# A gated hybrid layer: the first norm's 1/rms applied behind the projections, and x loaded already transposed

## The chip, the cores and the metric

The kernel runs on one core of one Trainium2 chip. The metric is the device time of one execution in microseconds (us). TensorE (PE in the profile) multiplies matrices, VectorE (DVE), ScalarE (ACT) and GpSimd (POOL) work on tiles, SyncE (SP) issues most of the transfers (DMAs).

## What is computed

One layer on x of 1024 tokens by 1024 channels, all in float32. Cut to what the change touches:

```python
h = rms_norm(x, norm1_w[l])
proj = h @ w_in[l]
q, k, v, g_ret, x_lru, y_lru, gate_ret, gate_lru = jnp.split(proj, SPLIT_POINTS, axis=-1)
q = rotary(q.reshape(bsz, seq, RET_HEADS, RET_DK), positions)
k = rotary(k.reshape(bsz, seq, RET_HEADS, RET_DK), positions) * (RET_DK ** -0.5)
o = chunkwise_retention(q, k, v.reshape(bsz, seq, RET_HEADS, RET_DV))
o = head_group_norm(o, ret_gn_w[l])
y_a = (o * jax.nn.silu(g_ret)) @ w_ret_o[l]
xc = causal_depthwise_conv(x_lru, lru_conv_w[l], lru_conv_b[l])
hl = rg_lru(xc, ...)
y_b = (hl * jax.nn.gelu(y_lru)) @ w_lru_o[l]
mix = (jax.nn.sigmoid(gate_ret + merge_gate_b[l, 0]) * y_a
       + jax.nn.sigmoid(gate_lru + merge_gate_b[l, 1]) * y_b)
x = x + mix @ w_out[l]
...
```

Behind these lines stand a second rms norm, a gated MLP with a short convolution, its residual and a final rms norm.

`rms_norm` is x * rsqrt(mean(x*x) + eps) * w, the mean over a row; `proj` has 7168 columns. Each row (token) of `h` is a row of x times one number, its 1/rms, and each column times a weight of the norm. A row's number can therefore multiply the product instead of x.

## The kernel before

**Numbers.** A float32 operand is split in two parts, hi and lo, of a shorter float type that TensorE takes in one pass: `split` (lines 167 and 168) casts hi on ScalarE and subtracts it on VectorE for lo. A product is three passes, hi by hi, hi by lo and lo by hi (`PASSES`).

**Jobs.** The first projection has 7168 columns. 256 of them make a job, so there are 28 jobs, in the order of `SEQ`: g is a merge gate, y the GeLU branch, h0 to h3 the four heads with three jobs each (q and k; v; the swish gate), x the LRU branch. A job has four weight blocks of 128 x 512 (`A11` to `A22`, column half and row half), and the operand `h1` has 32 tiles of 128 channels by 512 tokens, as 16 pairs of hi and lo: `B11` is the first four row tiles of channels and the first half of the tokens, `B12` the second half of the tokens, `B21` and `B22` the other four row tiles. The weights are the stationary side; the result has channels on the partitions and tokens along the row.

The first two jobs (`STD_L = 2`) are plain products, `mm_std`, of 96 matmuls (line 317): for each column half m it takes two PSUM banks, one for each half of the tokens. The others are `mm_fast`, which forms a job from seven smaller products of 12 matmuls (line 347) with sums of blocks: sums of weights are made by `preps` (S1 to S4, on VectorE, lines 235 to 251), and sums of the operand once by `tsets` (T1 to T4, lines 484 to 493), out of the unsplit tiles in `keep`. A fast job uses three banks, X, Y and Z; its partial results are copied out by ScalarE (line 362) and completed by VectorE (`total`, line 371).

**What a job does with its results.** `jb.emit(m, h, src, unit)` is called for each quarter. `src` is a PSUM bank or an SBUF tile (`unit`, then both are the same). `emit_gate` applies the sigmoid and stores, `emit_y` GeLU and stores, `emit_to` keeps a tile for the work behind (with a function for the swish gate). The work behind a job, retention, rotary, the LRU block, is a generator in `back`, which `advance` moves on between products.

**Order.** The program is written as one stream; a scheduler in the framework orders the instructions of each engine by priority (the place in the stream, moved ahead by 1500 inside `hp()`) and by the time at which it expects them to be ready. Each engine then works through its list in order. Weights are loaded (`loads`, line 197) and prepared (`preps`) ahead by `pump`, up to 7 prepared blocks. `Units` hands out the SBUF tiles of 2 KB a partition (`NU` of them in `u`, 22 in `w`) and the PSUM banks: six in `g` for products, two in `a` for everything else.

**The start.** x is loaded with tokens on the partitions (`xload`, line 503), eight tiles for each half of the tokens. `norm_half` forms the rows' 1/rms (`rms_scale`, squares on lines 440 and 442, the root and its refinement on lines 427 to 432), multiplies the tiles by it (line 455), transposes them on TensorE (line 462, with the identity out of `cst`), and makes from each transposed tile hi, lo and the unsplit tile, with the norm's weight as a scale for each partition (lines 466 to 472). The first half's norm uses all eight banks (`wide`) and stands ahead of the first job; the second half's comes into the first job's matmuls. The rotary tables are worked out on VectorE behind the second job (lines 541 to 600).

Of the kernel before, what the change touches and what calls it, by code (L numbers as in the profile page):

```python
# [11 lines left out]
F32 = mybir.dt.float32  # L12
# [74 lines left out]
class Units:  # L87
    """places of one shape in a pool, handed out oldest first in program order"""
# [23 lines left out]
NU = 78  # L112
# [16 lines left out]
def tile_trunk_layer(ctx, tc, x, positions, params, consts, normf, w_in, w_ro, w_lo,  # L129
# [34 lines left out]
    def split(src, get=get):  # L164
        """the two float32r parts of a float32 operand"""
        hi, lo = get(F32R), get(F32R)
        S.copy(hi, src)  # L167
        V.tensor_sub(lo, src, hi.bitcast(F32))  # L168
        return hi, lo
# [5 lines left out]
    ORD_T = ("A11", "A12", "A21", "A22")  # L175

    class Job:
        def __init__(self, src, op, emit, post=None, fast=False, last=False, drop12=False,
                     pre=None):
# [8 lines left out]
    def loads():  # L188
        i = 0
        while True:  # L190
            while i >= len(queue):
                yield None
            jb = queue[i]
            for nm in (("A11", "A21", "A22", "A12") if jb.fast else ORD_T):
# [18 lines left out]
    def preps():  # L213
        i = 0
        while True:
            while i >= len(queue):
                yield None
            jb = queue[i]

            def fin(nm, src):  # L220
                jb.blk[nm] = split(src, W.get)
                state["blocks"] += 1

            if not jb.fast:
                for nm in ORD_T:
# [110 lines left out]

    def mm_fast(jb, op):
# [56 lines left out]
    def run(jobs):  # L394
        if jobs[0] not in queue:
            queue.extend(jobs)
        pump()
        ahead = None
        for jb, nx in zip(jobs, jobs[1:] + [None]):
            state["hp"] = jb is not queue[0]  # L400
            if jb.fast:
# [9 lines left out]
                next(g, None)  # L411
            else:
# [21 lines left out]
    def rms_scale(tiles, n, o=0):  # L434
        """1 / rms of n token tiles, one column each"""
# [15 lines left out]
    def norm_half(tiles, wname, op, half, keep, wide=False):  # L451
# [4 lines left out]
        banks = [psg.get() for _ in range(len(psg))] if wide else []  # L456
        banks += [psa.get() for _ in range(len(psa))]
        for k in range(KT):
# [16 lines left out]
            if k + len(banks) >= KT:  # L475
                (psa if k % len(banks) >= len(banks) - 2 else psg).put(ps)
# [57 lines left out]
    rot = {}  # L534

    def rotary_tables():
# [55 lines left out]
        for hf in range(2):  # L592
# [13 lines left out]
    def emit_to(d, func=None):  # L606
        def emit(m, h, src, unit):
            t = get() if unit is None else unit
            if func is not None:
                S.activation(t, src, func)  # L610
            elif unit is None:
                S.copy(t, src)
            d[m, h] = t
        return emit

    def emit_y(n):
        def emit(m, h, src, unit):
            t = get() if unit is None else unit
            S.activation(t, src, AF.Gelu_apprx_tanh)
# [118 lines left out]
    def retention_head(hd, qk, vv):  # L738
        cur = 0
        mask = cst[:, C_MASK + 128 * hd:C_MASK + 128 * hd + 128]  # L740
        for h in range(2):
            for g in range(2):
# [7 lines left out]
                S.copy(t, ps)  # L750
# [64 lines left out]
    def emit_gate(which, n):  # L815
        def emit(m, h, src, unit):
            t = get() if unit is None else unit
            S.activation(t, src, AF.Sigmoid, bias=pc("merge_gate_b", 8 * which + 2 * n + m))
# [4 lines left out]
    def operand(op, fetch, sums=True):  # L823
        """the sets of an operand: first those of the plain product, then the sums"""
# [52 lines left out]
    def add(i, emit, post=None):  # L877
# [4 lines left out]
        jobs.append(Job(pair_src(w_in, i), h1, emit, post, fast=fastj(), drop12=len(jobs) == STD_L - 1))  # L882
# [7 lines left out]
    for what in SEQ.split():  # L890
# [5 lines left out]
        elif what[0] == "x":  # L896
            n = int(what[1])
            add(2 * n, emit_to(xl), lambda n=n: lru_block(n, dict(xl)))
        else:
# [4 lines left out]
            add(base + 2, emit_to(gg, AF.Silu), lambda hd=hd: ret_out(hd, dict(gg)))  # L904
# [22 lines left out]
    V.memset(st, 1.0)  # L927
    S.activation(st[:, 0:1], st[:, 1:2], AF.Sqrt)
# [8 lines left out]
    pump()  # L937
# [137 lines left out]
    def square(m, c):  # L1075
        """what a finished tile adds to its rows' sum of squares; then the norm's weights"""
# [40 lines left out]
def _pairs(w, cols):  # L1117
    """[pair, 2 * (column half) + row half, partition, (row tile, column)]"""
# [4 lines left out]
def _layout(inputs):  # L1123
# [8 lines left out]
    for n in range(8):  # L1132
# [8 lines left out]
        "x": c(a["x"][0]),  # L1141
        "positions": c(a["positions"]),
# [26 lines left out]
```

## Time and profile before

| | us |
|---|---|
| median of 3 runs | 1692.53 |
| lowest and highest run | 1690.29, 1696.99 |
| span of the profiled execution, first to last instruction | 1689.3 |
| TensorE busy in it | 1634.8 |
| VectorE busy | 1253.0 |
| ScalarE busy | 882.4 |
| mean granted TensorE clock | 0.992 |

The profile records one execution. No time of its own stands beside its span; the fastest timed run is 1.0 us above the span and the median 3.2 us. In the profile an instruction group is named by its line, its engine, the operation and `out<-in`; numbers of buffers are left out, so `u` is any of the 2 KB tiles, `g` a product bank, `w` a weight tile, `a` one of the two other banks. A matmul's duration (0.39 us) is longer than the distance to the next one, because they overlap in the array; the distance sets the pace.

### The profile page before, as it was taken

Reading aid. Unit: us, or ns where it says so; the run is one execution under the profiler, and the core shown is the slowest. Engines: PE = TensorE matmul, PEld = TensorE weight load, DVE = VectorE, ACT = ScalarE, POOL = GpSimd, SP = SyncE. Lnnn points to the kernel's source line nnn. Section 1 sums busy time; section 2 is a strip of 40 time slices with the busy share of each in tenths; the row PEclk is TensorE's granted clock in tenths of the full one; section 3 lists DMA queues with packets and bytes.
Section 4 is the critical chain, followed back from the end, with each engine's and each line's share of the span. In section 5 each row is a group of like instructions: output and inputs, shape, how many; then the busy total and the mean of one; then the engine's idle time right before and its main releaser. Section 6 shows DMA issues by size and latency. Waiting matters only on the chain. (4 is left out here: it accounts for less than half of the span.)

```text
span 1689.3 us, 21180 instructions
## 1 busy us (share of the span) xinstructions
PE 1634.8 (97%) x7284; PEld 1341.8 (79%) x7284; DVE 1253.0 (74%) x2295; ACT 882.4 (52%) x1464; POOL 40.7 (2%) x60
## 2 busy tenths in 40 slices
PE   6999999999999999999999999999999999999997
PEld 5888888878887887878778788888888887777776
DVE  7986676675677878758871797677766778878786
ACT  6663434445578978743440465444444455444454
POOL 0010000000000000000000001000000000000000
PEclk9999999999999999999999999999999999999999
DMA  5243132231333427457553123222222236686852
GB/s 191 94 143 94 35 97 79 60 88 50 100 107 106 144 100 268 162 193 243 175 181 115 66 75 95 87 81 82 82 87 82 84 122 230 225 268 219 265 196 81
DMA packets 118220, 221.78 MB, mean 131 GB/s; under 512 B 13792, under 2 KB 13920, under 8 KB 118112
## 3 DMA queue, kind: packets, MB, share of 16 engines
q1 hardware_dynamic: 113888, 206.79, 37.3%
q0 software_dynamic: 4224, 13.64, 2.8%
q8 instruction: 57, 0.93, 0.2%
q14 instruction: 51, 0.42, 0.1%
HBM read 160.60 MB, written 54.53 MB: 127 GB/s over the span
## 5 line engine op out<-in xcount | busy, mean ns | idle before, releaser
L347 PE MATMUL g<-u,w 128*128 128x512 f32 x5124 | 1208.3, 394 | 23.8 <-ACT u L362 16.9
L347 PEld LDWEIGHTS g<-u,w 128*128 128x128 f32 x5124 | 962.0, 189 | 228.9 <-ACT u L362 22.7
L167 ACT CAST w<-w 128x512 fp32r<-128x512 f32 x471 | 290.7, 621 | 374.0 <-PE g L347 288.8
L168 DVE TENSOR_TENSOR w<-w,w 128x512 fp32r<-128x512 f32 x471 | 322.3, 686 | 97.0 <-ACT w L167 88.7
L317 PE MATMUL g<-u,w 128*128 128x512 f32 x1056 | 248.7, 392 | 0.0
L317 PEld LDWEIGHTS g<-u,w 128*128 128x128 f32 x1056 | 197.4, 188 | 41.7 <-ACT u L466 1.2
L167 ACT CAST u<-u 128x512 fp32r<-128x512 f32 x232 | 141.0, 620 | 164.1 <-DMA u<-w_dn 29.1
L168 DVE TENSOR_TENSOR u<-u,u 128x512 fp32r<-128x512 f32 x232 | 154.5, 686 | 31.8 <-ACT u L167 25.1
L371 DVE TENSOR_TENSOR u<-g,u 128x512 f32<-128x512 f32 x183 | 125.9, 688 | 69.1 <-PE g L347 48.8
L362 ACT COPY u<-g 128x512 f32<-128x512 f32 x183 | 106.4, 581 | 72.2 <-PE g L347 71.0
L968 PE MATMUL g<-u,u 128*128 128x512 f32 x384 | 89.6, 392 | 1.0 <-ACT u L167 1.0
L968 PEld LDWEIGHTS g<-u,u 128*128 128x128 f32 x384 | 71.6, 188 | 15.9 <-ACT u L167 1.4
L1001 DVE SCALAR_TENSOR_TENSOR u<-u,par,u 128x511 f32<-128x511 f32 (+1 forms) x96 | 71.7, 748 | 6.4 <-ACT u L998 5.6
L1006 POOL DMA_DIRECT2D ff_d<-u x48 | 36.1, 753 | 1296.0 <-DVE u L1005 1287.6
L235 DVE TENSOR_TENSOR w<-w,w 128x512 f32<-128x512 f32 x61 | 42.1, 690 | 21.5 <-DMA w<-w_up 9.2
L660 PE MATMUL a<-u,u 128*128 128x512 f32 x192 | 49.1, 401 | 3.9 <-ACT u L663 2.4
L998 ACT ACTIVATE u<-u,par 128x512 f32<-128x512 f32 x48 | 39.2, 816 | 18.6 <-DVE u L371 16.4
L660 PEld LDWEIGHTS a<-u,u 128*128 128x128 f32 x192 | 36.8, 194 | 12.9 <-ACT u L663 2.8
L970 DVE TENSOR_TENSOR u<-g,u 128x512 f32<-128x512 f32 x16 | 11.1, 691 | 47.2 <-PE g L968 47.2
L238 DVE TENSOR_TENSOR w<-w,w 128x512 f32<-128x512 f32 x61 | 42.0, 688 | 1.0
L244 DVE TENSOR_TENSOR w<-w,w 128x512 f32<-128x512 f32 x61 | 41.9, 687 | 0.6
L251 DVE TENSOR_TENSOR w<-w,w 128x512 f32<-128x512 f32 x61 | 41.9, 686 | 0.4
(160 smaller groups left out, 1073.2 us busy)
## 6 DMA issues: line engine op xcount, KB each, us to landing
w<-w_in SPq DMA_DIRECT2D x112, 256.0 KB, 2.6
w<-w_up SPq DMA_DIRECT2D x96, 256.0 KB, 2.6
u<-w_dn SPq DMA_DIRECT2D x96, 256.0 KB, 4.1
u<-x_d SPq DMA_DIRECT2D x56, 256.0 KB, 4.1
x_d<-u SPq DMA_DIRECT2D x48, 256.0 KB, 3.3
ff_d<-u POOLq DMA_DIRECT2D x48, 256.0 KB, 2.7
w<-ff_d SPq DMA_DIRECT2D x48, 256.0 KB, 3.8
u<-x SPq DMA_DIRECT2D x32, 256.0 KB, 5.2
```

What stands on the lines that cost most here:

```text
L167: S.copy(hi, src)
L168: V.tensor_sub(lo, src, hi.bitcast(F32))
L235: V.tensor_add(s1, a21, a22)
L238: V.tensor_sub(s1, s1, a11)
L244: V.tensor_sub(a11, a11, a21)
L317: PE.matmul(ps[h], w[a][:, c], o[b], start=n == 0, stop=n == 23)
L347: PE.matmul(bank, w[a][:, c], need(op, (bn, j))[b], start=first and n == 0, stop=n == 11, skip_group_check=True)
L362: S.copy(u, bank)
L371: V.tensor_add(u, bank, u)
L660: PE.matmul(ps, wg[g][a][:, cs], xs[k][b], start=q == 0, stop=q == 5)
L968: PE.matmul(ps, o[a][:, 128 * t:128 * t + 128], wo[k][b], start=n == 0, stop=n == 23)
L1001: V.scalar_tensor_tensor(c[:, s:], src[:, :TH - s], w, c[:, s:], ALU.mult, ALU.add)
```

## The change

x is also handed over transposed, as eight row tiles of 128 channels by 1024 tokens (`xt`, made when the inputs are laid out). The first job's operand is made from these tiles without 1/rms: hi by ScalarE with the norm's weight as the scale, lo by VectorE. The loads of the first weight blocks and of the tiles of `xt` are mixed in the order of their use, and the first job runs through a new `mm_first`: for each half of the tokens it goes over the row tiles k and takes both column halves for each, with four banks open in all. Its block order is A11, A21, A12, A22.

x with tokens on the partitions is still loaded, behind that, for the sums of squares. 1/rms is kept in two forms: `rcol`, a column for 128 tokens, and `rbc[h]`, the row of 512 numbers repeated on all partitions, made by a float32 product of a matrix of ones with diagonal blocks. The unsplit tiles for `tsets` are the loaded tiles, multiplied by the norm's weight in place (`x_keep`).

Each result of the projections is multiplied by `rbc[h]` on VectorE before its function (gates, GeLU, swish, LRU branch); for q and k the rotary tables are multiplied instead, and v takes its factor from `rcol` when it is copied after its transposition, in two halves. There are three more SBUF tiles, for which the space of GpSimd's DMA descriptors is made smaller.

In the diff below, the two `tensor_mul` with `c` and `s` are in `rotary_tables`, the Gelu lines in `emit_y` (`emit_gate` is changed likewise), the scaled copy in `retention_head`; of the first half's sets only the first is shown, the others follow in the order of the loads.

```diff
-NU = 78
+NU = 81
...
+            self.order = order or (("A11", "A21", "A22", "A12") if fast else ORD_T)
...
+    def mm_first(jb, op, between):
+        banks = {}
+        for h in range(2):
+            for m in range(2):
+                banks[m, h] = psg.get()
+            for k in range(KT):
+                for m in range(2):
+                    an = f"A{m + 1}{k // 4 + 1}"
+                    pump((jb, an))
+                    w = jb.blk[an]
+                    c = slice(128 * (k % 4), 128 * (k % 4) + 128)
+                    o = op[f"B{k // 4 + 1}{h + 1}", k % 4]
+                    for n, (a, b) in enumerate(PASSES):
+                        PE.matmul(banks[m, h], w[a][:, c], o[b], start=k == 0 and n == 0,
+                                  stop=k == KT - 1 and n == 2)
+            between(h)
+        for nm in jb.order:
+            W.put(*jb.blk[nm])
+            state["blocks"] -= 1
+        for h in range(2):
+            for m in range(2):
+                jb.emit(m, h, banks[m, h], None)
+                psg.put(banks[m, h])
...
+    def x_set(k, h, b):
+        w = pc("norm1_w", k)
+        hi, lo = get(F32R), get(F32R)
+        S.activation(hi, b, AF.Copy, scale=w)
+        V.scalar_tensor_tensor(lo, b, w, hi.bitcast(F32), ALU.mult, ALU.subtract)
+        key = f"B{k // 4 + 1}{h + 1}", k % 4
+        h1[key] = (hi, lo)
+        keep[key] = b
+
+    def x_keep(h):
+        for k in range(KT):
+            b = keep[f"B{k // 4 + 1}{h + 1}", k % 4]
+            S.activation(b, b, AF.Copy, scale=pc("norm1_w", k))
+
+    def x_rms(tiles, h):
+        r = rms_scale(tiles, 4)
+        for t in tiles.values():
+            put(t)
+        V.tensor_copy(rcol[:, 4 * h:4 * h + 4], r)
+        diag = get()
+        for t in range(4):
+            V.tensor_scalar(diag[:, 128 * t:128 * t + 128], ident, r[:, t:t + 1], None, ALU.mult)
+        ps = psa.get()
+        PE.matmul(ps, ones, diag, start=True, stop=True)
+        put(diag)
+        t = get()
+        S.copy(t, ps)
+        psa.put(ps)
+        rbc[h] = t
...
+            V.tensor_mul(c, c, rbc[hf])
+            V.tensor_mul(s, s, rbc[hf])
...
-    def emit_to(d, func=None):
+    def emit_to(d, func=None, scaled=False):
         def emit(m, h, src, unit):
             t = get() if unit is None else unit
+            if scaled:
+                V.tensor_mul(t, src, rbc[h])
+                src, unit = t, t
             if func is not None:
                 S.activation(t, src, func)
...
-            S.activation(t, src, AF.Gelu_apprx_tanh)
+            V.tensor_mul(t, src, rbc[h])
+            S.activation(t, t, AF.Gelu_apprx_tanh)
...
-                S.copy(t, ps)
+                for b in range(2):
+                    cs = slice(256 * b, 256 * b + 256)
+                    n = 4 * h + 2 * g + b
+                    S.activation(t[:, cs], ps[:, cs], AF.Copy, scale=rcol[:, n:n + 1])
...
-    tl = xload(0)
     queue.extend(jobs)
-    for _ in range(4):
-        next(state["load"])
+    SY.dma_start(par, params)
+    xs = {}
+
+    def xget(k, h):
+        b = get()
+        SY.dma_start(b, xt[k, :, TH * h:TH * h + TH])
+        xs[k, h] = b
+
+    next(state["load"])
+    xget(0, 0)
+    next(state["load"])
+    for k in (1, 2, 3):
+        xget(k, 0)
+    next(state["load"])
+    next(state["load"])
+    for k in range(4, KT):
+        xget(k, 0)
+    for k in range(KT):
+        xget(k, 1)
     SY.dma_start(cst, consts)
-    SY.dma_start(par, params)
-    tl2 = xload(1)
-    norm_half(tl, "norm1_w", h1, 0, keep, True)
-    pump()
-    norm_half(tl2, "norm1_w", h1, 1, keep)
-    builders.append(tsets(h1, lambda n, j: keep[n, j]))
-    run(jobs)
+    next(state["prep"])
+    x_set(0, 0, xs[0, 0])
...
+    def between(h):
+        if h == 0:
+            for k in range(KT):
+                x_set(k, 1, xs[k, 1])
+            return
+        tl = xload(0)
+        pump()
+        x_keep(0)
+        x_keep(1)
+        x_rms(tl, 0)
+        x_rms(xload(1), 1)
+        builders.append(tsets(h1, lambda n, j: keep[n, j]))
+
+    run(jobs, between)
+    put(rbc[0], rbc[1])
...
-    nc = bacc.Bacc("TRN2", target_bir_lowering=False, num_devices=1)
+    nc = bacc.Bacc("TRN2", target_bir_lowering=False, num_devices=1, dynamic_dma_scratch_size=8192)
```

More of the change, by code (lines that the diff above doesn't have):

```diff
@@ L224, in preps @@
             if not jb.fast:
-                for nm in ORD_T:
+                for nm in jb.order:
                     fin(nm, raw(jb, nm))
@@ L335, in mm_std @@
                 drop(op.pop(("B12", j)))
+    def mm_first(jb, op, between):
[14 more added lines that the diff above has]
+            between(h)
+        for nm in jb.order:
+            W.put(*jb.blk[nm])
[4 more added lines that the diff above has]
+                psg.put(banks[m, h])
     def mm_fast(jb, op):
@@ L392, in mm_fast, with run @@
         psg.put(Z)
-    def run(jobs):
+    def run(jobs, between=None):
         if jobs[0] not in queue:
             queue.extend(jobs)
-        pump()
+        if between is None:
+            pump()
         ahead = None
@@ L411, in run @@
                 next(g, None)
+            elif between is not None and jb is jobs[0]:
+                mm_first(jb, jb.op, between)
             else:
@@ L449, in rms_scale, with norm_half @@
         return r
-    def norm_half(tiles, wname, op, half, keep, wide=False):
+    def norm_half(tiles, wname, op, half, keep):
         r = rms_scale(tiles, 4)
@@ L455, in norm_half @@
                 V.tensor_scalar(tiles[t, c], tiles[t, c], r[:, t:t + 1], None, ALU.mult)
-        banks = [psg.get() for _ in range(len(psg))] if wide else []
-        banks += [psa.get() for _ in range(len(psa))]
+        banks = [psa.get() for _ in range(len(psa))]
         for k in range(KT):
@@ L507, in tile_trunk_layer @@
     h1, keep = {}, {}
+    rbc = {}
+    rcol = pool.tile([P, 8], F32, tag="rcol", name="rcol")
+    ones = pool.tile([P, P], F32, tag="ones", name="ones")
+    def x_set(k, h, b):
[23 more added lines that the diff above has]
+        S.copy(t, ps)
+        psa.put(ps)
+        rbc[h] = t
     lt = pool.tile([P, 2, 8], F32, tag="lt", name="lt")
@@ L881, in post @@
                 return rotary_tables()
-        jobs.append(Job(pair_src(w_in, i), h1, emit, post, fast=fastj(), drop12=len(jobs) == STD_L - 1))
+        jobs.append(Job(pair_src(w_in, i), h1, emit, post, fast=fastj(), drop12=len(jobs) == STD_L - 1,
+                        order=None if jobs else ("A11", "A21", "A12", "A22")))
     gates = [(w, n) for n in range(4) for w in range(2)]
```

24 lines of the change are left out of this document (16 added, 8 removed).

## The prediction

> **What bounds the kernel now.** I read the page's engine shares first, then TensorE's waits, then the order of time at the start, then busy time by stretch.
>
> ```profile
> span 1689.3 us, 21180 instructions
> PE 1634.8 (97%) x7284; PEld 1341.8 (79%) x7284; DVE 1253.0 (74%) x2295; ACT 882.4 (52%) x1464; POOL 40.7 (2%) x60
> PE g L347 <- ACT u L362: 16.9, 9, 2.9
> PE g L462 <- DVE u L455: 14.7, 1, 14.7
> 150.00:650.00 500.00, 496.46 (x2296) 409.90 (x2295) 358.01 (x703) 295.88 (x462) 0.00 (x0) 1.00 0.29 92
> 450.00:650.00 200.00, 198.49 (x876) 164.04 (x875) 154.80 (x260) 162.43 (x232) 0.00 (x0) 1.00 0.37 125
> 550.00:600.00 50.00, 50.00 (x223) 41.38 (x222) 43.58 (x74) 45.26 (x66) 0.00 (x0) 1.00 0.38 132
> ```
>
> The last three are stretches; after the length come the busy times of PE, PEld, DVE, ACT and POOL. TensorE (PE) is the limit: 1634.8 of 1689.3 us. Its longest single wait is 14.7 us, the start, for the scaled rows that the first transposes read. From 150 to 650 us, which is most of the input projections, it idles 3.5 us. So the kernel gets faster only by starting TensorE's real work earlier or by taking work from it; and VectorE (DVE), 358 of 500 us there and 155 of 200 us late in it, has little room for more before it takes TensorE's place. The start in order of time (start, duration):
>
> ```profile
> 0.74 3.71 SPq L503 DMA_DIRECT2D u<-x  x8
> 3.42 0.60 ACT L440 ACTIVATE a<-u 128x512 f32<-128x512 f32 x1 [1.19 <-DMA u<-x]
> 4.08 0.70 DVE L442 SCALAR_TENSOR_TENSOR a<-u 128x512 f32<-128x512 f32 x1 [3.19 <-DMA u<-x]
> 5.33 0.60 ACT L440 ACTIVATE a<-u 128x512 f32<-128x512 f32 x1 [1.19 <-DMA u<-x]
> 7.15 0.70 DVE L442 SCALAR_TENSOR_TENSOR a<-u 128x512 f32<-128x512 f32 x1 [2.31 <-DMA u<-x]
> 9.83 0.70 DVE L442 SCALAR_TENSOR_TENSOR a<-u 128x512 f32<-128x512 f32 x1 [0.60 <-DMA u<-x]
> 10.44 0.62 ACT L167 CAST w<-w 128x512 fp32r<-128x512 f32 x1 [0.57 <-DMA w<-w_in]
> 14.69 4.92 PE L462 MATMUL g<-cst,u 128*128 128x128 f32 x24 [14.69 <-DVE u L455]
> 20.23 11.14 PE L317 MATMUL g<-u,w 128*128 128x512 f32 x48
> 47.23 21.72 PE L317 MATMUL g<-u,w 128*128 128x512 f32 x94
> 68.79 41.42 PE L347 MATMUL g<-u,w 128*128 128x512 f32 x182
> ```
>
> Loads of 256 KB land one by one: the first by 3.42 us, the second by 4.08, third 5.33, fourth 7.15, eighth 9.83, ninth (the first weights) 10.44; later ones 0.67 us apart ((9.83 - 7.15) / 4). The first product matmul starts at 20.23 us. The first two jobs, 2 x 96 = 192 matmuls on line 317, end at 68.79 us, where the fast jobs begin. Matmuls are issued 0.227 us apart ((41.42 - 0.39) / 181, with 0.39 us the duration of one), so 192 need 43.5 us; 68.79 - 20.23 = 48.6 us were spent, the other 5 us on the second half's transposes and short waits.
>
> **The change, part by part.**
>
> The start. SP now issues the parameters (100 KB, 0.4 of a tile), one weight block, one tile of transposed x, the second block, three more tiles of x, two blocks, and so on. By the landings above, counted in tiles of 256 KB and interpolated, the first x tile (2.4 tiles) is in at about 4.6 us, the second block (3.4) at 6.0, the second x tile (4.4) at 7.4, and each later one 0.67 us after the last. ScalarE's set (hi) takes 0.69 us, so the first matmul starts at about 5.3 us, and the second row tile k = 1 at 8.1 us. From there TensorE is the slower side: a k has 2 x 3 matmuls, 1.36 us, against 0.67 us for its tile. VectorE's part of a tile, 0.75 us, fits under it as well:
>
> ```profile
> L467 DVE SCALAR_TENSOR_TENSOR u<-a,par,u 128x512 fp32r<-128x512 f32 x13 | 9.7, 748 | 0.5 <-ACT u L466 0.4
> L466 ACT ACTIVATE u<-a,par 128x512 fp32r<-128x512 f32 x13 | 9.0, 693 | 13.6 <-PE a L462 13.6
> 18.00:19.00 1.00, 1.00 (x7) 1.00 1.05 387
> 19.00:20.00 1.00, 1.00 (x12) 1.00 1.04 385
> ```
>
> The two stretches are TensorE alone: 7 transposes in the microsecond from 18, 12 in the next. So it works at about half speed for its first 4.3 us (14.69 to 19). Before, that falls on transposes; after, on matmuls, from 5.3 to about 9.6 us. Most of it lies in the wait for k = 1; what is left is three matmuls at twice 0.227 us, 0.7 us. Then k = 1 ends at 10.1 us, the other 6 k of the first half at 18.3, the second half (48 matmuls, 10.9 us) at 29.2, job 1 (21.8 us) at 51.0.
>
> The Trainium skill, TensorE: Matmul & The Clock Gate, Part 1, says that the array starts at half clock and gets the full one after a window of about 3.4 us of sustained work, and that matmuls separated by load waits can keep it cold. By that rule the gate would open only after k = 1 is under way, near 12 us, and the start would cost some 2 us more (an estimate), 1685 in place of the sum's result; the trace agrees on the half speed, and no row here shows a gate held shut by waits.
>
> The rms now runs beside the products. Its 64 transposes go (32 of them between the matmuls of job 0). TensorE gets instead two products of 128x512 in plain float32 for the row of 1/rms. The nearest rows:
>
> ```profile
> 204.80 0.59 PE L778 MATMUL a<-u,u 128*128 128x256 f32 x2
> 205.04 0.58 PE L347 MATMUL g<-u,w 128*128 128x512 f32 x1
> ```
>
> One float32 product of 256 columns is two records and holds TensorE 0.24 us, so two of 512 columns about 1.0 us. The fast jobs would begin at 52.0 instead of 68.8 us: 16.8 us won if nothing else is late.
>
> What is late next. The fast jobs need the operand sums (T1 to T4), and VectorE and ScalarE make them:
>
> ```profile
> 20.20:68.80 48.60, 48.28 (x228) 38.95 (x227) 47.51 (x98) 36.11 (x64) 0.00 (x0) 1.00 0.25 86
> 48.21 1.90 DVE L168 TENSOR_TENSOR u<-u,u 128x512 fp32r<-128x512 f32 x3
> L440 ACT ACTIVATE a<-u 128x512 f32<-128x512 f32 x16 | 9.8, 614 | 34.9 <-DMA u<-x_d 30.0 <-DMA u<-x 4.7
> L818 ACT ACT_TABLE_LOAD x10 | 12.8, 1283 | 0.2
> ```
>
> VectorE is busy 47.5 of the 48.6 us before the fast jobs. VectorE's instructions start 0.60 us apart ((1.90 - 0.69) / 2). After, it has, up to the last T4: 16 low parts of x, 8 of weights, 8 squares, 32 for the sums (16 differences, 16 low parts), 8 new multiplications for jobs 0 and 1, 11 for the first fast weights: 83 at about 0.63 us, and some 24 small ones at 0.18, or 56.6 us. Starting at 5 us and never waiting, it ends at 61.6. T1's last part is wanted at about 57 us and T4's first at 65.6 (2.7 us a product), and T1's last lies about 5 us ahead of the end, so there is no slack. ScalarE has 16 high parts, 16 rescalings of x in place, 8 casts of weights, 8 squares, 16 high parts of sums, 8 emits, 7 fast weights, 2 copies: 81 at some 0.57 us, and 5 table loads of 1.28, 53 us in the same stretch. Two engines so full, each waiting for the other in order, will lose something. Bounds: nothing, or a tenth of both queues one after the other, 10 us. I take 4 us, nearer to nothing because VectorE now starts 5 us earlier than at present and the rotary work, which fills it after 57 us, can wait.
>
> The multiplication by 1/rms waits for both norms' chain (loads of x behind all the others, squares, root, product, copy), some 35 to 40 us. Behind job 0's multiplications stand its four banks; six are there, so job 1 takes the other two, and its second half needs a bank at 29.2 + 10.9 = 40 us. If the multiplication comes later, TensorE waits; that is within the 10 us, since a wait here gives the sums their time.
>
> The rest of the projections. Of 28 jobs, 20 are multiplied, 4 results each: 80 new VectorE instructions, 72 behind the first two jobs, 43 us at 0.60. They are no TensorE work; where VectorE has room they are hidden. In 450 to 650 us some ten such jobs add 24 us to 154.8: 179 of 200. In 550 to 600 us, 6 us to 43.58: 49.6 of 50. The X bank's result is now read by VectorE, not ScalarE, and ScalarE's function waits for one more instruction, with the copies that free X (line 362) queued behind. Bounds: nothing (VectorE's backlog moves into the idle time beside it) or all of the ten jobs' 28 us (40 x 0.69). I take 3 us, since TensorE idles 1.5 us there now and the mean stays under 90%.
>
> Free: v's copy as two scaled halves, 16 x (2 x 0.37 - 0.59) = 2.4 us of ScalarE, by
>
> ```profile
> L774 ACT COPY u<-a 128x256 f32<-128x256 f32 x32 | 11.8, 370 | 35.1 <-PE a L769 33.3 <-PE a L767 1.8
> L750 ACT COPY u<-a 128x512 f32<-128x512 f32 x16 | 8.6, 591 | 0.4
> L1006 POOL DMA_DIRECT2D ff_d<-u x48 | 36.1, 753 | 1296.0 <-DVE u L1005 1287.6
> ```
>
> under matmuls of 0.227 us in a stretch where ScalarE has 296 of 500 us; uncovered it would cost those 2.4. The smaller scratch for POOL's DMAs: 48 issues of 0.75 us and 1296 us of waiting for data, so two at a time at most; nothing. Three more places, less two held by the rows of 1/rms: nothing. The 4 MB loaded twice: DMA share 0.25 in that stretch; nothing behind the first 30 us.
>
> Sum: 16.8 - 4 - 3 = 9.8 us, and 1689.3 - 9.8 = 1679.5 of span. The median of the runs is 3.2 us above the span, so 1682.7: **1683 us**.
>
> **The rivals.** *All is hidden:* both losses are nothing; 16.8 us, 1676. For it: TensorE waited 3.5 us in 500. Against: VectorE's full 47.5 of 48.6 us. Chance 0.18.
>
> *The queues jam early:* the sums or 1/rms come 10 us late and the gain is 16.8 - 10 - 3 = 4: 1689. For it: the counts of 56.6 and 53 us, with T1 at no slack. Chance 0.22.
>
> *The start isn't early:* the program orders sets or loads so that k = 1 and later starve, the first product ends 5 us later: 5 us less, 1688. Against: landings 0.67 us apart. Chance 0.05.
>
> *VectorE becomes the bound in the LRU stretch:* from 450 us on, each multiplied job grows by its four multiplications, 2.8 us; ten jobs give 28 in place of the 3: 1683 + 25 = 1708. It decides once VectorE, or ScalarE waiting for it (162 of 200 already), has no idle time over more than one job, which 550 to 600 us reaches by the sum. Against: the blocks of weights are prepared a job ahead, 19 us of cushion. Chance 0.15.
>
> **How the numbers follow.** Forecast 0.40, its own range 1679 to 1688. About 0.5% (8.5 us) is what a measurement of this kernel can tell from no change: faster is below 1684.1, slower above 1701. Faster: 0.18 and 0.29 of the forecast's 0.40 and 0.03 of the two small gains: 0.50. Slower: 0.15. Within: 0.35. The range runs from under the all-hidden case, 1674, to 1698, leaving out the VectorE case and a little below.
>
> **What would show it.** First line-317-like matmul near 5.3 us and no L462 transposes before 600 us; 192 matmuls done and the fast jobs begun at 52 to 58 us; VectorE over 95% busy from 10 to 60 us; its busy time in a fast gate job up by 2.4 us; TensorE idle in the projections behind that under 8 us. Wrong if the fast jobs begin after 62 us, or if TensorE's idle time from 70 to 640 us exceeds 15 us with VectorE or ScalarE named as releaser.

## The result, and the profile after

The changed kernel takes 1702.38 us (median of 6 runs, 1698.53 to 1705.09); the kernel before, run beside it, 1691.87 (6 runs). The ratio is 1.0056, interval 1.0041 to 1.0072: some 9.5 us slower, where 1683 us was forecast. The profiled execution of after took 1698.53 us, the fastest of its six; of its span:

```profile
span 1696.8 us, 21199 instructions
PE 1635.3 (96%) x7224; PEld 1337.2 (79%) x7224; DVE 1293.3 (76%) x2366; ACT 891.0 (53%) x1485; POOL 40.7 (2%) x60
```

TensorE's busy time is that of before (1634.8), the span is 7.5 us longer: by this count all that is lost is waiting. (The count hides that the 64 transposes of the first norm are gone and that some matmuls ran slower; the last section shows where.) TensorE's order of time at the start, in the trace of after (start, duration, engine, line, operation, how many, idle time before it and its releaser):

```profile
5.61 24.87 PE L352 MATMUL g<-u,w 128*128 128x512 f32 x96 [5.61 <-ACT u L546]
30.32 11.04 PE L318 MATMUL g<-u,w 128*128 128x512 f32 x48
49.90 2.04 PE L566 MATMUL a<-u,ones 128*128 128x512 f32 x2 [8.54 <-DVE u L564]
53.96 13.43 PE L318 MATMUL g<-u,w 128*128 128x512 f32 x48 [2.01 <-DVE u L891]
67.23 2.43 PE L373 MATMUL g<-u,w 128*128 128x512 f32 x10
70.83 1.12 PE L566 MATMUL a<-u,ones 128*128 128x512 f32 x2 [1.18 <-DVE u L564]
74.74 20.52 PE L373 MATMUL g<-u,w 128*128 128x512 f32 x81 [2.78 <-DVE u L891]
```

Line 352 is the new first product (job 0), 318 the plain one (317 before), 373 the fast jobs (347 before), 566 the product with ones that spreads 1/rms, 891 the multiplication of a gate's result by it. The first product starts and ends early as meant. Then come two holes, one at 41.36 us (30.32 + 11.04), one at 69.66, and both end at an instruction of the 1/rms chain. TensorE's waits in the first 100 us, all of them:

```profile
PE a L566 <- DVE u L564: 9.7, 2, 8.5
PE g L352 <- ACT u L546: 5.6, 1, 5.6
PE g L373 <- DVE u L891: 2.8, 1, 2.8
PE g L318 <- DVE u L891: 2.0, 1, 2.0
```

To see where a gain goes I count 6564 product matmuls in each trace (lines 352, 318, 373 and 1078, or 317, 347 and 968; 1078 and 968 are the product with `w_out`) and compare the start of the n-th, counted from 0, with that of before. Negative is ahead, in us:

| n | 96 | 192 | 240 | 576 | 3200 | 6000 | 6400 | last |
|---|---|---|---|---|---|---|---|---|
| before, start of the n-th | 46.4 | 68.8 | 79.7 | 155.8 | 884.3 | 1546.1 | 1642.7 | 1680.7 |
| after | -16.1 | -1.6 | +5.5 | +5.7 | +6.3 | +3.2 | +7.2 | +7.6 |
| after, second execution (e13) | -15.2 | -0.5 | +7.1 | +7.3 | +5.7 | +4.4 | +12.2 | +12.7 |
| after, third execution (e14) | -16.2 | -1.7 | +5.3 | +5.6 | +3.6 | +1.5 | +8.0 | +8.5 |
| before, second execution (e15) | +0.9 | +0.9 | +0.9 | +0.9 | +2.0 | +0.1 | +1.1 | +1.9 |

So 16 us are won by the 96th product, and 21 to 22 us are lost between it and the 240th. A second loss, of 4 to 8 us, lies between the 6000th and the 6400th.

**Why 1/rms came late.** VectorE in the trace of after, first the first square of the first half's chain, then its end, with what became of it on ScalarE (the copy of the row) and VectorE:

```profile
35.14 0.69 DVE L471 SCALAR_TENSOR_TENSOR a<-u 128x512 f32<-128x512 f32 x1
45.15 0.68 DVE L512 TENSOR_TENSOR u<-u,u 128x512 f32<-128x512 f32 x1
45.75 0.17 DVE L457 RECIPROCAL nst<-nst 128x4 f32<-128x4 f32 x1
45.84 0.46 DVE L609 TENSOR_SCALAR u<-u,cst 128x512 f32<-128x512 f32 x1
46.21 0.69 DVE L518 TENSOR_TENSOR u<-u,u 128x512 f32<-128x512 f32 x1
46.81 0.16 DVE L458 TENSOR_TENSOR nst<-nst 128x4 f32<-128x4 f32 x1
46.88 0.42 DVE L612 TENSOR_SCALAR u<-u 128x512 f32<-128x512 f32 x1
47.22 0.16 DVE L459 TENSOR_TENSOR nst<-nst 128x4 f32<-128x4 f32 x1
48.89 0.87 DVE L564 TENSOR_SCALAR u<-cst,nst 128x128 f32<-128x128 f32 x4
51.98 0.59 ACT L569 COPY u<-a 128x512 f32<-128x512 f32 x1 [5.18 <-PE a L566]
53.22 0.69 DVE L891 TENSOR_TENSOR u<-g,u 128x512 f32<-128x512 f32 x1
```

Lines 457 to 461 are the root's refinement, 0.16 us each, one depending on the other. Between two of them stands a big instruction of the sums (512, 518) or of the rotary tables (609, 612), which nobody waits for at this time. What would be about 1 us takes from 45.75 to 49. The squares before it (line 471) alternated with the sums in the same way and, above all, began late: x for them was the last of SyncE's loads at the start (issued from 19.3 to 30.0 us), the eight tiles of the first half had landed between 24.5 and 30.0 us, and the first square on VectorE stands at 35.14, the last at 40.34. Half 0's row of 1/rms was there at 52.6 us, and VectorE's first multiplication of a gate's result stands at 53.22. Until then job 0 held its four banks and job 1's first half the other two: no bank for job 1's second half.

Half 1 was worse. Its last squares stand behind the product with ones (line 471 writes its squares to one of the two `a` banks), its Sqrt on ScalarE behind casts that wait for TensorE. ScalarE in the trace of after:

```profile
58.61 0.62 ACT L167 CAST u<-u 128x512 fp32r<-128x512 f32 x1 [0.26 <-DMA sg_d<-u]
62.44 0.62 ACT L167 CAST u<-u 128x512 fp32r<-128x512 f32 x1 [3.21 <-PE g L318]
63.08 1.28 ACT L456 ACT_TABLE_LOAD   x1
64.38 0.21 ACT L456 ACTIVATE nst<-nst 128x4 f32<-128x4 f32 x1
```

So TensorE waited for 1/rms, and 1/rms waited for TensorE.

### The profile page after: what moved, and what is told of

It is laid out like the page before. It is cut to its first block, busy times and chain, and to the rows that moved or that the text cites. A ratio compares the mean times of both kernels' runs of the same rounds, so it can differ in the third digit from the quotient of the medians.

```text
span 1696.8 us, 21199 instructions
## 1 busy us (share of the span) xinstructions
PE 1635.3 (96%) x7224; PEld 1337.2 (79%) x7224; DVE 1293.3 (76%) x2366; ACT 891.0 (53%) x1485; POOL 40.7 (2%) x60
## 4 chain that ended last, share of the span: by engine, by line
issue 77%; PE 12%; DVE 3%; DMA 3%; POOL 2%; ACT 1%; SPq 0%; POOLq 0%; DVEq 0%; ACTq 0%
PE g L373 9%; PE g L318 3%; POOL ff_d L1116 2%; DMA u<-w_dn 1%; DMA w<-ff_d 1%; DVE u L168 1%; DVE w L168 0%; DMA ff_d<-u 0%; DVE u L1172 0%; ACT u L167 0%; DMA x_d<-u 0%; DVE u L397 0%; DVE u L512 0%; DMA u<-x_d 0%; ACT u L388 0%
## 5 line engine op out<-in xcount | busy, mean ns | idle before, releaser
L373 PE MATMUL g<-u,w 128*128 128x512 f32 x5124 | 1211.9, 395 | 24.5 <-ACT u L388 16.4
L373 PEld LDWEIGHTS g<-u,w 128*128 128x128 f32 x5124 | 963.6, 189 | 231.2 <-ACT u L388 22.2
L318 PE MATMUL g<-u,w 128*128 128x512 f32 x960 | 227.0, 394 | 5.9 <-DVE u L168 2.5
L318 PEld LDWEIGHTS g<-u,w 128*128 128x128 f32 x960 | 181.0, 190 | 47.0 <-DVE u L891 3.6
L1111 DVE SCALAR_TENSOR_TENSOR u<-u,par,u 128x511 f32<-128x511 f32 x96 | 71.6, 747 | 5.9 <-ACT u L1108 5.2
L1108 ACT ACTIVATE u<-u,par 128x512 f32<-128x512 f32 x48 | 39.1, 817 | 16.5 <-DVE u L397 16.5
```

Of the source, the lines that this page charges most:

```text
L318: PE.matmul(ps[h], w[a][:, c], o[b], start=n == 0, stop=n == 23)
L373: PE.matmul(bank, w[a][:, c], need(op, (bn, j))[b], start=first and n == 0, stop=n == 11, skip_group_check=True)
L1111: V.scalar_tensor_tensor(c[:, s:], src[:, :TH - s], w, c[:, s:], ALU.mult, ALU.add)
```

## The experiments

Kernels that were measured together share the runs of the kernel before, so times are compared by their ratio to it.

**Without the chain (e4).** Rows and column of 1/rms are set to 1, so this kernel leaves out the first norm's scaling:

```diff
-        x_rms(tl, 0)
-        x_rms(xload(1), 1)
+        put(*tl.values())
+        put(*xload(1).values())
+        for h in range(2):
+            rbc[h] = get()
+            V.memset(rbc[h], 1.0)
+        V.memset(rcol, 1.0)
```

> The changed kernel without the chain of 1/rms: the factors are set to one, so the first norm's scaling is left out; loads, sums, products and all multiplications stay. Theory 1 (TensorE's early wait is for 1/rms alone, because job 0's four banks wait for it): the fast jobs begin at 52 to 55 us instead of 67, the wait of 21 us is gone and the time is about 1681 us, some 10 below the kernel before. Theory 2 (VectorE's work for the operand sums is the bound, in whatever order): the first fast job waits for its sums instead, the 240th product matmul starts after 75 us (85 in the changed kernel, 79.7 before), time about 1692. Theory 3 (the multiplications cost in the rest of the projections): the gain at the 240th matmul melts away up to the 2400th.

1678.14 us, ratio 0.9909 (0.9887 to 0.9932). TensorE in its trace:

```profile
7.47 23.24 PE L352 MATMUL g<-u,w 128*128 128x512 f32 x95 [1.02 <-ACT w L167]
30.55 21.92 PE L318 MATMUL g<-u,w 128*128 128x512 f32 x96
52.31 43.00 PE L373 MATMUL g<-u,w 128*128 128x512 f32 x189
```

No hole; the fast jobs begin at 52.31 us, and the gain (16.5 us at the 240th product) doesn't melt away behind it (13.5 at the 2400th, 18.3 at the 3200th), as theory 1 has it and theory 3 does not. The sums are not late, though VectorE is busy 31.86 of the 32 us from 20 to 52 us. One rival is left open here: VectorE and ScalarE have lost the chain's own work too (the squares, and on VectorE the small steps). The version e8 below does all this work, and the sums aren't late there either. The early loss is the chain's.

**The chain ahead (e1).** Both `x_rms` under high priority:

```diff
-        x_rms(tl, 0)
-        x_rms(xload(1), 1)
+        tl2 = xload(1)
+        with hp():
+            x_rms(tl, 0)
+            x_rms(tl2, 1)
```

> The changed kernel with the instructions of the 1/rms chain at the priority that the operand sums have (loads unchanged). Theory 1: squares go as the loads of x land (by 33 us), the row of 1/rms is ready for the first half at about 42 us and for the second at 45 to 50, TensorE waits under 3 us in job 1; fast jobs begin at 53 to 57 us, time about 1684 us. Theory 2: the sums are now late by what the chain takes, 6 to 8 us of VectorE, and the 240th product matmul still starts after 75 us; time 1690 to 1695.

1692.81 us, ratio 0.9999 (0.9985 to 1.0012): the loss is gone, the gain isn't there. The product with ones now ran at 41.50 us, yet the hole stayed, by TensorE's waits and rows of VectorE's order of time in this trace:

```profile
PE g L318 <- DVE u L891: 9.6, 1, 9.6
29.64 0.69 DVE L471 SCALAR_TENSOR_TENSOR a<-u 128x512 f32<-128x512 f32 x1
37.05 0.17 DVE L457 RECIPROCAL nst<-nst 128x4 f32<-128x4 f32 x1
40.48 0.87 DVE L564 TENSOR_SCALAR u<-cst,nst 128x128 f32<-128x128 f32 x4
51.46 0.68 DVE L891 TENSOR_TENSOR u<-g,u 128x512 f32<-128x512 f32 x1
```

These rows also say what the priority changed: the squares begin 5.5 us earlier (29.64, not 35.14) and the steps between them and the reciprocal are faster, but from the reciprocal to the diagonal (line 564) the chain takes as long as before, 3.4 us in place of 3.1. So the 8.4 us by which the product with ones came earlier were not lost between the steps of the refinement, but ahead of them.

The row was there at 43.2 us, but job 0's multiplication, at its plain place, came behind the sums and the second half's chain, 8 us later. The 240th product starts at 77.3 us and the time is inside theory 2's range, but not by its cause: TensorE waits 0.5 us for the sums and 9.6 for the multiplication. A chain is as late as its last member.

**Copies out of the first banks (e7).** ScalarE copies the first two jobs' results to SBUF at once, so their banks don't wait for 1/rms:

```diff
+            if early:
+                with hp():
+                    S.copy(t, src)
+                src = t
             V.tensor_mul(t, src, rbc[h])
```

> The changed kernel with the results of the first two jobs copied out of their banks by ScalarE before the multiplication (8 copies of 0.58 us); the chain of 1/rms is left as slow as it is. Theory 1, narrowed to the banks (job 1's second half waits only because job 0's banks wait for their multiplications): no wait of TensorE for the multiplication in job 1, fast jobs begin at 53 to 56 us, time 1685 to 1688 us. Rival (the product with the matrix of ones stands in TensorE's own list ahead of job 1's second half, and is itself waiting for the diagonal): TensorE still waits 6 us or more for the diagonal, fast jobs begin after 60 us, time about 1695 us.

1700.82 us, ratio 1.0044 (1.0027 to 1.0062). At the 192nd product it is 17.0 us ahead, at the 240th 14.9, by the 288th 2.9 behind. The longest of TensorE's waits behind the start, in its first 100 us:

```profile
PE g L373 <- DVE u L168: 8.3, 2, 7.9
PE g L373 <- ACT u L167: 3.7, 2, 2.4
```

The banks were what job 1 waited for (the fast jobs begin at 51.78 us, so theory 1 has the place right and the rival falls), but the time is neither theory's. The wait moved by one job: the second half's product with ones (at 71.64 us) stands in TensorE's list among the first fast jobs, ScalarE waits for it with a copy out of a bank (2.85 us) and copies the row behind that, and the last sums come later still. Freeing the bank alone changes only where TensorE stops.

**One chain for both halves: alone, ahead, and with the copies (e3, e2, e8).** `rms_scale` takes all eight token tiles at once, so the root and its refinement are done once, with 128x8 numbers:

```diff
-    def x_rms(tiles, h):
-        r = rms_scale(tiles, 4)
+    def x_rms(tiles):
+        r = rms_scale(tiles, 8)
```

> One chain for both halves at its plain priority, without copies: it shows what the second chain by itself costs. Theory E (the second half's own chain, which came 20 us behind the first, made most of the +5.5 us at the 240th product): no wait of the first fast job for it, the 240th product 0 to 3 us behind the kernel before or ahead of it, 1694 to 1699. Theory F (the place of the chain behind the sums counts, not their number): the 240th product 5 us behind or more, 1701 to 1705.

> One chain of 1/rms for both halves under high priority, without ScalarE's copies: the first job's four banks are held until its multiplications. Theory C (both cures are needed): job 1's second half still waits for the first job's banks, as with two chains under high priority: the 192nd product at 63 to 67 us, the 240th 0 to 4 us ahead of the kernel before, 1690 to 1694. Theory D (the single chain does it, since the multiplications come right behind it): the 192nd product at 53 to 58 us, the 240th 10 to 14 us ahead, 1684 to 1687.

> The changed kernel with the copies of the last kernel, one chain of 1/rms for both halves in place of two, and the chain at the priority of the operand sums. Theory 1: neither the banks nor the product with ones hold TensorE; fast jobs begin at 53 to 55 us, the 240th product matmul starts at 64 to 66, time 1680 to 1684 us, below both kernels. Theory 2 (VectorE's work for the sums): 240th after 72 us, time about 1690.

| | ratio | interval | start of the 192nd, us | 240th against before |
|---|---|---|---|---|
| e3: one chain, plain priority | 1.0033 | 1.0020 to 1.0047 | 74.9 | +6.1 |
| e2: one chain, high priority | 0.9979 | 0.9963 to 0.9995 | 65.1 | -3.7 |
| e8: the same and the copies | 0.9954 | 0.9939 to 0.9969 | 53.7 | -14.9 |

At plain priority one chain is no cure: its product with ones came at 56.68 us (idle before it 14.87), and the place in the lists counts, not the number of chains (F by the progress, though its time, 5.6 us over before, is less than F's 9 to 13). Ahead, it still leaves 7.2 us of waiting for it, and 1.5 for the multiplication (C by the progress; the profiled execution, 1693.40 us, was the longest of its ten, so the median is better than that trace). With the copies there is next to nothing left before the fast jobs; TensorE in the trace of e8:

```profile
30.02 17.61 PE L318 MATMUL g<-u,w 128*128 128x512 f32 x77
47.57 1.95 PE L567 MATMUL a<-u,ones 128*128 128x512 f32 x4
48.96 4.88 PE L318 MATMUL g<-u,w 128*128 128x512 f32 x19
53.68 14.24 PE L373 MATMUL g<-u,w 128*128 128x512 f32 x61
```

The chain's small steps still alternate with the sums in it, and nobody waits for them. Two chains ahead with the copies were not run, so what the single chain adds to those two cures isn't known; without the copies, one chain ahead (e2) is 0.9979 and two ahead (e1) 0.9999. e8 is 15 us ahead at the 240th product, but only about 8 us faster (0.0046 x 1692.9): the rest is lost later.

**The multiplications (e5)** and **the space (e6, e9, e10)**, each put into the kernel before, alone:

```diff
+            if scaled:
+                V.tensor_mul(t, src, rbc)
+                src, unit = t, t
```

> The kernel before with the 80 multiplications alone (by a tile of ones, so the results are unchanged): nothing else of the change. Theories 1 and 2: hidden, within 2 us of the kernel before, 1690 to 1694 us. Theory 3: 10 to 28 us slower, from the LRU stretch on (from the 1500th product matmul).

1694.38 us, ratio 1.0010 (0.9997 to 1.0024): 1.7 us at most likely, 4 at the bound. The 80 multiplications are hidden, all or nearly all.

```diff
-NU = 78
+NU = 81
...
-    nc = bacc.Bacc("TRN2", target_bir_lowering=False, num_devices=1)
+    nc = bacc.Bacc("TRN2", target_bir_lowering=False, num_devices=1, dynamic_dma_scratch_size=8192)
```

> The kernel before with 81 tiles and the smaller descriptor space alone. All theories: nothing, within 3 us of the kernel before. If the smaller space delays GpSimd's transfers, the writes of ff_d take longer to land than 2.7 us and the stretch from 1000 us on grows.

1702.88 us, ratio 1.0058 (1.0040 to 1.0077), a surprise: three tiles more, and no other edit but the room for them, cost the kernel before as much as the whole change. Which of the two lines, and is it the threshold of 20 free tiles (`RESERVE`) from which an operand is begun early?

> The kernel before with the smaller descriptor space alone (78 tiles). If the space itself costs: 1700 to 1704 us, as with space and tiles together. If the three tiles cost, because operands are built earlier and the order of the instructions changes: 1690 to 1694, as before.

> The kernel before with the smaller space and 81 tiles, of which the builder of operands must leave 23 free in place of 20, so that it starts as early as with 78. If the tiles cost by letting operands be built earlier: back to 1690 to 1694 us. If they cost in another way (which tile follows which), or the space does: still 1698 to 1704.

The smaller scratch alone (78 tiles): 1691.92 us, ratio 0.9995 (0.9975 to 1.0014), nothing. The tiles with a threshold of 23: 1695.05 us, ratio 1.0012 (0.9996 to 1.0029), nearly all given back. That looked like the cause, so the threshold was raised in the changed kernel and in e8:

> The changed kernel with one number different: a projection's operands are begun with 23 free tiles instead of 20, the kernel before's own margin counted for the three tiles that the change adds. Theory A (the loss has two parts that add: some 6 us in the first 80 us, by the chain of 1/rms, and some 5 us at the end, by operands that start earlier because more tiles are free): the first 600 products as in the changed kernel (about +5.7 us against the kernel before at the 576th), and a median of 1695 to 1699, 1697 most likely. Theory B (the early chain alone makes the loss, and the space only took effect in the kernel before, with its other order of the start): no difference from the changed kernel, 1701 to 1704. If under 1693, the early loss doesn't reach the end.

> The version with one chain of 1/rms under high priority and ScalarE's copies out of the first banks, with the 23 free tiles. Theory A: its early gain of 14 us is kept to the end instead of 6 to 7: 1677 to 1681, 1679 most likely. Theory B: 1685, as with 20.

Ratios 1.0056 (1.0036 to 1.0077) and 0.9950 (0.9931 to 0.9970): the same as with 20. My theory of the threshold fell. In the kernel before it gains 3.2 us up to the 6000th product (against e6's trace), and the loss from there to the last is with it (6.6 us) about what it was without (7.2); by which order of the lists it gains was not tried.

**More executions (e13, e14, e15).** Is the rest of the loss in the first 80 us of other executions, or later?

> The changed kernel as it is, a second profiled execution. Theory G (the part of the loss that the first profile doesn't show, some 4 us of 9.5, is in the first 80 us: the chain of 1/rms comes later in other executions): the 576th product 8 to 12 us behind the kernel before's 155.8 us. Theory H (it is lost later, in the stretches with much transfer): the 576th product 3 to 6 us behind in this execution too, whatever its whole time.

> The same once more, a third execution: theory G 8 to 12 us behind at the 576th product, theory H 3 to 6 us.

> The kernel before, a second profiled execution, against which the two are read. Both theories: its 576th product within 1 us of 155.8 us, since it waits for nothing behind the 96th; the progress behind the 600th shows how far single executions of one kernel swing there: under 2 us for theory G, 4 us or more for theory H.

Both stretches, by the table above: 5.3 to 7.1 us behind at the 240th product, 5.6 and 7.3 at the 576th, less than theory G wanted, and a step of 4 to 8 us between the 6000th and the 6400th that the kernel before's second execution doesn't have (1.0). TensorE's waits for the copies of partial results (line 362 before, 388 after) in the last 240 us, first before, then after, then e6:

```profile
PE g L347 <- ACT u L362: 5.9, 4, 1.9
```

```profile
PE g L373 <- ACT u L388: 10.8, 8, 3.1
```

```profile
PE g L347 <- ACT u L362: 11.5, 5, 3.8
```

In the thirteen traces with 81 tiles to the end (after three times, e1 to e4, e6 to e8, e10 to e12) that group is 9.5 to 12.8 us, in the four with 78 (before twice, e5, e9) 5.9 to 8.3. ScalarE's own waits in the same stretch, before and after:

```profile
ACT u L167 <- DMA u<-w_dn: 21.3, 14, 2.8
```

```profile
ACT u L167 <- DMA u<-w_dn: 31.8, 18, 4.7
```

ScalarE casts weights of the last stage that have not landed (27.2 to 35.4 us of waiting with 81 tiles, 21.3 to 25.1 with 78), and its list is worked through in order, so a copy for TensorE that stands behind such a cast is late. That this makes the whole difference is not shown.

**Three tiles out of use behind the projections (e16, e17, e18).** One line, where the projections end, in the changed kernel, in e8 and in e6:

```diff
     put(rbc[0], rbc[1])
+    held = [get() for _ in range(3)]
```

> The changed kernel, with three of the 81 tiles taken out of use when the projections are done, so that the rest of the kernel has 78 as the kernel before. Theory I (the loss at the end goes with the three tiles: in the kernels with 81 TensorE waits 9.5 to 12.2 us in the last 240 us for the copies of the bank results, line 388 or 362, in those with 78 5.9 to 6.9 us): that wait back at 6 to 7 us, the loss at the start unchanged (3 to 7 us at the 576th product), 4 us less in all: a ratio of 1.0025 to 1.004. Theory J (any change of the order behind the projections does it, and the number of tiles is chance): the wait stays at 9 us or more, a ratio of 1.005 to 1.006.

> The version with one chain of 1/rms under high priority and ScalarE's copies out of the first banks, with the three tiles taken out behind the projections. Theory I: its early gain of 14 us reaches the end but for 2 or 3 us: a ratio of 0.9920 to 0.9935. Theory J: 0.995 as without.

> The kernel before with 81 tiles in the projections and 78 behind them. Theory I: most of the 10 us that the three tiles cost it are lost behind the projections: a ratio of 1.000 to 1.002. Theory J: 1.005 to 1.006, as with 81 throughout.

| | ratio with 81 | ratio with 78 behind the projections | interval |
|---|---|---|---|
| changed kernel (e16) | 1.0056 | 1.0017 | 1.0002 to 1.0033 |
| one chain, ahead, and copies (e17) | 0.9954 | 0.9919 | 0.9894 to 0.9944 |
| kernel before with 81 in the projections (e18) | 1.0058 | 0.9998 | 0.9982 to 1.0014 |

Three times 6 to 10 us come back, and most of the wait in the last 240 us with them; in e16:

```profile
PE g L373 <- ACT u L388: 6.1, 6, 1.5
ACT u L167 <- DMA u<-w_dn: 23.5, 13, 3.7
```

(8.0 us in e17, 7.4 in e18.) The progress says the same over all twenty traces: from the 6000th product to the last, those with 81 tiles there lose 4.4 to 9.0 us against the kernel before's first trace, those with 78 there 0 to 3.6. So the tiles are the cause of the late loss; e16's early loss (6.9 us at the 240th product) is untouched. That they act through the order of the transfers and lists is likely but not shown: which transfer is put where by them was not followed further. The late loss needn't show in the time: e10 has it (6.6 us) and is 1.0012 in all, since it was ahead before.

e17 is the best version: 1679.49 us (6 runs, 1677.88 to 1684.29), some 13.7 us faster than the kernel before.

## Why the prediction was wrong

**The start: right.** First matmul 5.61 us (forecast 5.3), job 0 done at 30.3 (29.2). With the chain taken out (e4) the fast jobs begin at 52.31 us; the sum had 52.0 with nothing late. Of the 1.1 us between 29.2 and 30.3, 0.3 are the start; the rest, 0.8 us, is half speed beyond what was priced:

```profile
8.00:9.00 1.00, 1.00 (x4) 0.48 (x2) 0.71 (x2) 1.00 (x3) 0.00 (x0) 1.00 0.98 354
11.00:12.00 1.00, 1.00 (x6) 0.82 (x5) 1.00 (x3) 1.00 (x3) 0.00 (x0) 1.00 1.06 410
```

These are stretches of after; behind the length stand the busy times of PE, PEld, DVE, ACT, POOL (instructions in parentheses), the clock, the DMA share and GB/s. Four matmuls are under way in the ninth microsecond, six in the twelfth. In the same trace they start 0.427 us apart up to 10.96 us and 0.23 apart from 11.23, so the clock opened at about 11.1 us, not 9.6 (the clock column, 1.00, doesn't show this first stretch). And no wait for the second row tile hid the half speed: at that pace the first six matmuls lasted until 8.7 us, and the seventh followed without a gap. The Trainium skill's rule quoted in the prediction (TensorE: Matmul & The Clock Gate, Part 1) had the opening near 12 us and some 2 us of cost; the trace lies between that and my reading, nearer to the rule in the time and to my reading in the cost (0.8 us more than priced).

**"What is late next": the step that failed.** It took 4 us, with 10 as the bound. Measured from the 96th to the 240th product: 21.6 us (16.1 + 5.5). The fast jobs began at 67.23 us, which the prediction had named as proof against it (62). Of the 21.6, by the rows above, 14.5 are waits for VectorE's part of the chain (8.5, 2.0, 1.2, 2.8), 3.2 the products with ones themselves (2.04 and 1.12; the sum had 1.0), and some 4 the half clock that the idling brought back (2.4 of them in job 1's second half, 13.43 - 11.04, and 1.8 behind 74.74 us, where the matmuls up to the 240th took 10.4 us in place of 38 x 0.227 = 8.6; see the last section). The first product with ones ran at half clock as well: e1's takes 1.10 us. Two inputs of the step were wrong. The chain was put at "some 35 to 40 us", without a sum; it was 52.6 us for the first half and 72.6 for the second, because its squares, its small steps and its copies wait for whatever stands before them in the lists. And the bound of 10 us rested on "a wait here gives the sums their time"; but the sums didn't need it (e4 and e8 don't wait for them), and the wait has no such limit, since it ends with the chain and not with the sums. The named rival, the queues that jam ("the sums or 1/rms come 10 us late"), had the place right and, at 10 us, half the size.

**The 80 multiplications: right in kind, mis-sized.** 3 us taken; e5 gave 1.7. In the trace of after, behind the start:

```profile
156.00:656.00 500.00, 494.89 (x2284) 407.21 (x2283) 384.23 (x751) 293.84 (x470) 0.00 (x0) 1.00 0.29 90
556.00:606.00 50.00, 49.26 (x217) 40.32 (x216) 43.88 (x77) 42.53 (x62) 0.00 (x0) 1.00 0.38 127
```

VectorE 384.2 us in place of 358.0, and TensorE idles 5.1 us in place of 3.5. The tight stretch of the prediction, where its sum put VectorE at 49.6 of 50 us, shows 43.9 after the change (43.6 before): it was not made fuller there. Why was not followed. VectorE did not become the bound; the rival that had the right sign, with its 1708, was wrong in its mechanism.

**"Three more places: nothing": the second step that failed.** With the tiles taken back behind the projections the ratio falls from 1.0056 to 1.0017, 6.6 us (0.0039 x 1692). The sum had nothing for them. The prediction asked whether the space would be short, and not what a surplus does to an order that was settled for 78. The smaller scratch was nothing, as said (e9).

**The sum.** The early part gives 21.6 - 16.1 = 5.5 us lost, the multiplications 1.7, the tiles 6.6: 13.8, of which the median shows 9.5. About as much as is missing is made up in between: the changed kernel is 8.5 us behind at the 2400th product and 3.2 at the 6000th. Why was not tried; single executions of the kernel before differ there by 2 us.

## What to carry to other kernels

Moving a factor behind a product takes it off the product's start but not off the path: the banks are held until the factor is there, so follow the whole chain (last load, squares, the small steps, the spreading product, its copy, the multiplication) through each engine's list, and count for each small dependent step one big instruction ahead of it. Give such a chain its priority as a whole, from the first square to the last multiplication, and let the banks go without it; each cure by itself left TensorE a stop of 8 to 15 us (9.6 with the chain ahead, 8.3 with the copies, 14.9 with one chain at plain priority). And a buffer added for one stage can cost time in a later one: measure it by itself, and take it out of use where the stage ends.

## What the runs showed of the hardware

A long wait of TensorE costs more than its length. Stretches of after:

```profile
45.00:46.00 1.00, 0.00 (x0) 0.00 (x0) 1.00 (x4) 0.97 (x3) 0.00 (x0) 0.59 0.00 0
55.00:56.00 1.00, 1.00 (x4) 0.81 (x3) 1.00 (x4) 0.25 (x1) 0.00 (x0) 0.50 0.47 184
58.00:59.00 1.00, 1.00 (x4) 0.81 (x3) 0.96 (x4) 0.74 (x2) 0.00 (x0) 0.59 0.02 4
59.00:60.00 1.00, 1.00 (x6) 0.79 (x6) 0.98 (x4) 0.23 (x1) 0.00 (x0) 1.00 0.68 262
```

The granted clock (third from the right) falls to half some 4 us after the end of the last matmul (41.36), and is full again only at about 58.8, 4.9 us after job 1's matmuls went on at 53.96. Until then they start 0.427 us apart, then 0.227. Job 1's second half took 13.43 us where its first took 11.04. The Trainium skill, TensorE: Matmul & The Clock Gate, Part 1, gives an idle window of about 3.4 us for the fall and a busy one for the return; the trace agrees, with a return somewhat later than one window. The prediction priced its waits without such a fall.
